# First MLP's up projection by one level of a Strassen scheme, with the activations at another 64-byte offset in SBUF

## The chip, the cores and the metric

The kernel runs on one core of a Trainium2 chip. The metric is device time in microseconds (us) of one execution. The kernel before was timed in three runs: 1188.42 to 1190.4 us, median 1188.81 us. Every time below comes from these runs or from the profile of one execution of the kernel before.

## What is computed

The program is a trunk of two layers over 512 positions of width 1024, in float32. Cut to what matters here:

```python
def sq_relu_mlp(h, w1, w2):
    return jnp.square(jax.nn.relu(h @ w1)) @ w2      # w1: 1024 x 4096, w2: 4096 x 1024

for i in range(2):
    hn = rmsnorm(h, norm_mix_g[i])
    h = h + (dsa_mixer(hn, ...) if i == 0 else conv_mixer(hn, ...))
    h = h + sq_relu_mlp(rmsnorm(h, norm_mlp_g[i]), mlp_w1[i], mlp_w2[i])
return rmsnorm(h, final_g)
```

Layer 0 is attention and an MLP ("the first MLP"), layer 1 a convolution mixer and an MLP ("the second MLP"). The change rewrites the first half of the first MLP, `h @ w1`.

## The kernel before

**Layout.** The residual `hT` lies transposed: 8 tiles of 128 features by 512 positions. A product of fp32 matrices is made of three TensorE matmuls on split operands (`mm3`, L90 to L93): each operand is a high part and a low part, hi·hi, hi·lo and lo·hi are summed in PSUM. The activations' parts are the tiles `ghi` and `glo`, written by `scaled` (ACT L174, DVE L175); the weights' parts are `whi` (ACT L86) and `wlo` (DVE L87), made by `split` for 512 columns of a weight tile at a time. `load` (L76) brings 1 MB of weights by SP's queue into `wraw`, a pool of two buffers.

**The first MLP.** It goes in four groups of 1024 hidden features. In a group `up_proj` makes 8 blocks of 128 features, each 8 k-steps of three matmuls of 512 columns into one PSUM bank; `hidden` turns a block into its square with relu and the rms factor (DVE L636, ACT L638 and L641, DVE L642) and leaves it as a pair `hh`, `hl`. Then `proj` makes the group's part of the down projection in 8 blocks, and DVE adds each to `hT` (L709). The factor `rr` of the rms norm is worked out after the first block or two (`rms_cols`, `broadcast`: DVE L181, POOL, DVE L190, four small matmuls, ACT L193), because it is applied to the result. Splits go to the pool `wsplit_mid`, 12 buffers for each of the two parts.

**What sets the order.** TensorE runs the blocks as the code writes them. A scheduler puts ACT's and DVE's work in order, by its own simulated times; each engine then takes its instructions strictly in that order, and a later one can't pass an earlier one that waits. SP's queue issues the loads in order; a load waits until the buffer that it fills has been read for the last time.

**Around it.** Before the first MLP stands the end of the attention layer: `wo_end` adds the last output blocks to `hT` (L617) and calls `scaled` for each feature tile. Behind group 0 stands `stacked_taps`, which builds the convolution's diagonal weights on POOL (L700). The pools `att` (attention) and `mlp` (first MLP) lie over the same memory. In SBUF all activations and weights start at a multiple of 512 bytes.

Of the kernel before, what the change touches and what calls it, by code (L numbers as in the profile page):

```python
# [42 lines left out]

ROW = 512
FILL = 64
# [3 lines left out]
def kernel(  # L49
# [29 lines left out]
    wsplit = []  # L79

# [19 lines left out]
    def bank(name="mm"):  # L100
        return acc.tile([P, S], F32, tag="mm", name=name)
# [36 lines left out]

    fill = small.tile([P, FILL // 4], F32, name="fill")
    nc.gpsimd.memset(fill, 0.0)  # L140
# [79 lines left out]
    with tc.tile_pool(name="wsplit_att", bufs=5) as ws, \  # L220
# [3 lines left out]
        wsplit.append(ws)  # L224
# [193 lines left out]
        with tc.tile_pool(name="heads", bufs=1) as heads:  # L418
# [86 lines left out]
            with tc.tile_pool(name="att_p", bufs=2) as att_p:  # L505
# [110 lines left out]
                def wo_end(c, ps):  # L616
                    nc.vector.tensor_add(hT[c], ps, hT[c])  # L617
                    scaled(c, vec("mlp", c))
                    rms_add(st, c)
# [42 lines left out]
    def pw1_first(k):  # L662

        for i, p in enumerate((aproj, gproj)):
# [9 lines left out]
    diags = [late.tile([P, max(TAPS0[c][0], TAPS1.get(c, (0, 0))[0]), 4, 32], F32, name=f"diag{c}")  # L674
             for c in range(KC)]

    def stacked_taps(pool):
# [3 lines left out]
        cw4 = pool.tile([P, 2 * P], F32, name="cw4")  # L681
        sel = pool.tile([P, 32], F32, name="sel")
# [4 lines left out]
        for i in range(2):  # L687
            r = pool.tile([P, 4, 32], F32, name=f"cwr{i}")
# [14 lines left out]
    with tc.tile_pool(name="mlp", bufs=1) as mlp:  # L703
        rr = []
        for g in range(NG - 1):
            hid = up_proj(mlp_w1[0][:, g * D:(g + 1) * D], rr, mlp, st if g == 0 else None)
            down = proj(mlp_w2[0][g * D:(g + 1) * D, :], hid)
            for c in range(KC):
                nc.vector.tensor_add(hT[c], down([c])[0], hT[c])  # L709
            if g == 0:  # L710
                stacked_taps(mlp)
        hid = up_proj(mlp_w1[0][:, DFF - D:], rr, mlp)
        down = proj(mlp_w2[0][DFF - D:, :], hid)
# [17 lines left out]
    HS = S // 2  # L731
    halves = [slice(0, HS), slice(HS, S)]
    with tc.tile_pool(name="cv", bufs=1) as cv, \
# [7 lines left out]
        with tc.tile_pool(name="cv_t", bufs=2) as cv_t:  # L741
# [14 lines left out]
            def taps(c, cs, npe, npool):  # L756
# [16 lines left out]
                sh4 = cv_t.tile([P, 4, S + 4 * (TAPS // 4 - 1)], F32, tag="sh4", name="sh4")  # L773
# [265 lines left out]
```

## Time and profile before

| | |
|---|---|
| runs | 1188.42 to 1190.4 us, median 1188.81 us |
| profiled execution, own time | 1186.75 us |
| its span, first to last instruction | 1185.0 us |
| busy: TensorE (PE), DVE, ACT, POOL | 97%, 56%, 42%, 21% of the span |
| the first MLP | 274 us to about 636 us |

PE is matmuls, DVE the vector engine, ACT the scalar engine, POOL GpSimd, SP the engine that issues most DMAs. A row of the timeline is start, duration, engine, line, operation, output<-inputs; a number at the end (x8) is a run of the same instruction, and square brackets give the idle time ahead of it and what ended it. The profiled execution's own time is 1.75 us above its span, and 2.06 us below the median of the runs.

### The profile page before, as it was taken

The page shows a single profiled execution, that of the slowest core. Times are in us where ns is not written, and L with a number is a line of the kernel's source. Part 1 is how long each engine was busy: PE and PEld are TensorE (multiplying, and loading weights), DVE is VectorE, ACT ScalarE, POOL GpSimd, SP SyncE. Part 2 cuts the span into 40 slices and gives each one's busy share as a digit, 9 for nine tenths or more (in the row PEclk, how much of TensorE's full clock was granted, in tenths as well). Part 3 has the DMA queues.
Part 4 walks back from the last instruction along what each step waited for, and adds up shares of the span by engine and source line. Part 5 has one row for each costly group of instructions (what it writes and reads, how often), then busy time and mean ns, then how long its engine had stood idle before and what let it go on. Part 6 is the DMA issues. An engine that isn't in the chain of part 4 may idle for free.

```text
span 1185.0 us, 15284 instructions
## 1 busy us (share of the span) xinstructions
PE 1150.8 (97%) x5828; PEld 948.5 (80%) x5828; DVE 663.3 (56%) x1195; ACT 498.2 (42%) x936; POOL 247.5 (21%) x248
## 2 busy tenths in 40 slices
PE   7999999999999999999999988899999999999997
PEld 6778888877888888888888666689888888888886
DVE  4589854476434434434444998878544434434434
ACT  5353454545423423423435544466632432432422
POOL 2436643322005000000012667632100000000000
PEclk8999999999999999999999998999999999999999
DMA  6122222215233323322323563533322332332211
GB/s 229 36 71 72 89 84 77 71 36 182 78 100 107 98 80 107 107 83 78 125 71 116 151 172 91 161 108 115 117 86 92 107 107 72 106 107 92 86 36 71
DMA packets 104353, 117.84 MB, mean 99 GB/s; under 512 B 3817, under 2 KB 87609, under 8 KB 104280
## 3 DMA queue, kind: packets, MB, share of 16 engines
q1 hardware_dynamic: 102440, 112.89, 30.6%
q10 hardware_dynamic: 1840, 3.97, 0.9%
q8 instruction: 46, 0.75, 0.3%
q14 instruction: 27, 0.22, 0.1%
HBM read 112.56 MB, written 4.29 MB: 99 GB/s over the span
## 4 chain that ended last, share of the span: by engine, by line
PE 81%; DVE 12%; DMA 2%; issue 2%; ACT 1%; POOL 1%; SPq 0%; POOLq 0%; DVEq 0%; ACTq 0%
PE mm L91 19%; PE mm L93 19%; PE mm L92 19%; PE dps L93 5%; PE dps L92 5%; PE dps L91 5%; DVE score L482 2%; DVE m L480 2%; DVE conv L802 2%; DVE wlo L87 2%; DVE pa L798 1%; PE vps L91 1%; PE vps L92 1%; PE vps L93 1%; DMA xs<-in_x_dram 1%
## 5 line engine op out<-in xcount | busy, mean ns | idle before, releaser
L86 ACT ACTIVATE whi<-wraw 128x512 fp32r<-128x512 f32 x378 | 234.6, 631 | 469.9 <-PE mm L92 317.1
L92 PE MATMUL mm<-glo,whi 128*128 128x512 f32 (+1 forms) x928 | 337.0, 365 | 1.2 <-DVE glo L175 1.2
L93 PE MATMUL mm<-ghi,wlo 128*128 128x512 f32 (+1 forms) x928 | 337.1, 365 | 0.0
L91 PE MATMUL mm<-ghi,whi 128*128 128x512 f32 (+1 forms) x928 | 334.6, 366 | 1.9 <-ACT whi L86 0.8
L87 DVE TENSOR_TENSOR wlo<-wraw,whi 128x512 fp32r<-128x512 f32 x325 | 233.5, 726 | 177.7 <-ACT whi L86 174.1
L92 PEld LDWEIGHTS mm<-glo,whi 128*128 128x128 f32 x928 | 175.0, 189 | 31.0 <-issue 2.4
L91 PEld LDWEIGHTS mm<-ghi,whi 128*128 128x128 f32 x928 | 173.1, 189 | 32.6 <-issue 2.8
L93 PEld LDWEIGHTS mm<-ghi,wlo 128*128 128x128 f32 x928 | 175.0, 189 | 28.7 <-issue 1.1
L93 PE MATMUL mm<-hh,wlo 128*128 128x512 f32 x256 | 99.6, 389 | 0.0
L92 PE MATMUL mm<-hl,whi 128*128 128x512 f32 x256 | 99.6, 389 | 0.0
L92 PE MATMUL dps<-wlo,hh 128*128 128x512 f32 x256 | 99.6, 389 | 0.0
L91 PE MATMUL mm<-hh,whi 128*128 128x512 f32 x256 | 99.1, 389 | 0.0
L91 PE MATMUL dps<-whi,hh 128*128 128x512 f32 x256 | 99.1, 389 | 0.0
L93 PE MATMUL dps<-whi,hl 128*128 128x512 f32 x256 | 98.6, 389 | 0.0
L636 DVE SCALAR_TENSOR_TENSOR hr<-mm,rmsb 128x512 f32<-128x512 f32 x64 | 44.1, 691 | 91.9 <-PE mm L93 90.2
L87 POOL TENSOR_TENSOR wlo<-wraw,whi 128x512 fp32r<-128x512 f32 x53 | 70.9, 1342 | 89.6 <-ACT whi L86 89.5
L183 POOL TENSOR_TENSOR fr<-v,mhalf 128x1 f32<-128x1 f32 x4 | 2.2, 548 | 340.2 <-DVE v L181 340.2
L642 DVE TENSOR_TENSOR hl<-hf,hh 128x512 fp32r<-128x512 f32 x64 | 44.6, 697 | 41.9 <-ACT hh L641 41.9
L206 POOL TENSOR_TENSOR ss<-sq 128x512 f32<-128x512 f32 (+1 forms) x4 | 5.7, 1434 | 270.3 <-ACT sq L201 270.3
L790 POOL TENSOR_TENSOR pa<-pa,pt 128x512 f32<-128x512 f32 (+1 forms) x43 | 53.6, 1249 | 32.6 <-ACT pt L788 30.5
L92 PEld LDWEIGHTS mm<-hl,whi 128*128 128x128 f32 x256 | 48.0, 188 | 10.1
L92 PEld LDWEIGHTS dps<-wlo,hh 128*128 128x128 f32 x256 | 48.0, 188 | 10.0
(257 smaller groups left out, 1588.2 us busy)
## 6 DMA issues: line engine op xcount, KB each, us to landing
wraw<-in_mlp_w_dram SPq DMA_DIRECT2D x64, 1024.0 KB, 5.2
wraw<-in_conv_w_pw_dram SPq DMA_DIRECT2D x12, 1024.0 KB
wraw<-in_dsa_w_in_dram SPq DMA_DIRECT2D x10, 1024.0 KB, 9.1
wraw<-in_dsa_w_out_dram SPq DMA_DIRECT2D x4, 1024.0 KB, 4.9
sh<-flat SPq DMA_DIRECT2D x12, 260.0 KB, 3.6
sh<-flat SPq DMA_DIRECT2D x20, 138.0 KB, 2.8
xw<-in_dsa_w_in_dram ACTq DMA_DIRECT2D x4, 584.0 KB, 7.4
xs<-in_x_dram SPq DMA_DIRECT2D x4, 512.0 KB, 12.1
```

The lines of the kernel that those rows point to most:

```text
L86: nc.scalar.activation(hi, src, AF.Copy)
L87: (eng or nc.vector).tensor_sub(lo, src, hi.bitcast(F32))
L91: nc.tensor.matmul(ps, wh, xh, start=start, stop=False)
L92: nc.tensor.matmul(ps, wh, xl, start=False, stop=False)
L93: nc.tensor.matmul(ps, wl, xh, start=False, stop=stop)
L480: nc.vector.max(m8s[-1], score[i])
L482: nc.vector.match_replace(score[i], m8s[i - 1], score[i], TAKEN)
L636: nc.vector.scalar_tensor_tensor(r, ps, 0.0, rr[0], op0=OP.max, op1=OP.mult)
L642: nc.vector.tensor_sub(tl, f, th.bitcast(F32))
L790: nc.gpsimd.tensor_add(pa, pa, pt)
L798: nc.vector.scalar_tensor_tensor(pa, sh(t), wt(t), pa, op0=OP.mult, op1=OP.add)
L802: nc.vector.scalar_tensor_tensor(cps, sh(t), wt(t), cps, op0=OP.mult, op1=OP.add)
```

## The change

A Strassen scheme multiplies two matrices of 2 by 2 blocks with 7 block products in place of 8. Here the blocks are: two of the hidden features (128 each), two halves of the 1024 inputs (4 tiles of 128 each), and two halves of the 512 positions. `pair` handles two feature blocks: 7 products of 4 k-steps by three matmuls of 256 columns (84 matmuls of 256 columns, where two blocks had 48 of 512). `two_pairs` interleaves two pairs, in TensorE's order p1, q5 (pair a), p1, q5 (pair b), then p2, p2, q6, q6, p7, p7, p3, p4, p3, p4. Its operands are sums: on the weights' side four (s1 to s4, DVE, `plain`, 512 columns), of which each is split like a weight; on the activations' side d1, e2, e3 and e4, worked out once before group 0 by `first_half` and `second_half`, which take over the work of `scaled`. The products of a pair are put together again through copies out of PSUM on ACT and sums on DVE.

```diff
-FILL = 64
+SHIFT = 64
+HS = S // 2
...
+    def wsplit_pool(stack, name, bufs, fill):
+        pool = stack.enter_context(tc.tile_pool(name=name, bufs=bufs, side="right"))
...
+        nc.gpsimd.memset(pool.tile([P, fill // 4], F32, tag="fill", name="fill", bufs=1), 0.0)
...
-    fill = small.tile([P, FILL // 4], F32, name="fill")
-    nc.gpsimd.memset(fill, 0.0)
...
                 def wo_end(c, ps):
                     nc.vector.tensor_add(hT[c], ps, hT[c])
-                    scaled(c, vec("mlp", c))
                     rms_add(st, c)
...
-    wsplit.append(ctx.enter_context(tc.tile_pool(name="wsplit_mid", bufs=12)))
+    wsplit_pool(ctx, "wsplit_mid", 12, 32 + ROW - SHIFT)
...
-            if g == 0:
-                stacked_taps(mlp)
...
+        def first_half(i):
+            w = mlp.tile([P, S], F32, tag="hh", name="xa", bufs=8)
+            x12 = mlp.tile([P, S], F32, tag="hl", name="x12", bufs=8)[:, t1]
+            nc.scalar.activation(w[:, t1], hT[i][:, t1], AF.Copy, scale=vec("mlp", i))
+            nc.scalar.activation(x12, hT[i][:, t2], AF.Copy, scale=vec("mlp", i))
+            nc.vector.tensor_sub(w[:, t2], w[:, t1], x12)
+            nc.scalar.activation(ghi[i], w, AF.Copy)
+            nc.vector.tensor_sub(glo[i], w, ghi[i].bitcast(F32))
...
+        def second_half(i, d1, x12):
+            c = i + 4
+            x = mlp.tile([P, S], F32, tag="hr", name="xb", bufs=2)
+            nc.scalar.activation(x, hT[c], AF.Copy, scale=vec("mlp", c))
+            nc.scalar.activation(ghi[c], x, AF.Copy)
+            nc.vector.tensor_sub(glo[c], x, ghi[c].bitcast(F32))
...
+            nc.vector.tensor_add(v[:, 0], d1, x[:, t2])
+            nc.vector.tensor_sub(v[:, 1], x12, x[:, t2])
+            nc.vector.tensor_sub(v4, x[:, t1], v[:, 0])
+            hi, lo = triple(2 * i), triple(2 * i + 1)
+            for src, at in ((v, slice(0, 2)), (v4.unsqueeze(1), slice(2, 3))):
+                nc.scalar.activation(hi[:, at], src, AF.Copy, scale=-1.0)
+                nc.vector.scalar_tensor_tensor(lo[:, at], src, -1.0, hi[:, at].bitcast(F32),
+                                               op0=OP.mult, op1=OP.subtract)
...
+        PRODUCTS = {"p1": ("a11", "b11"), "p2": ("a12", "b21"), "q5": ("s1", "d1"), "q6": ("s2", "e2"),
+                    "p7": ("s3", "e3"), "p3": ("s4", "b22"), "p4": ("a22", "e4")}
+        def pair(w, p):
+            raw = load(w, 0, KC, 2 * p * P, 2 * P)
...
+            def plain(name):
+                of = {"s1": ("a21", "a22"), "s2": ("s1", "a11"), "s3": ("a21", "a11"), "s4": ("s2", "a12")}
+                if name not in a:
+                    x, y = (plain(n) for n in of[name])
+                    a[name] = mlp.tile([P, 4, P], F32, tag="cs", name="cs", bufs=5)
+                    nc.vector.tensor_add(a[name], x, y)
+                return a[name]
...
+        def two_pairs(w, p, hid, between=lambda: None):
+            prods = [pair(w, p + z) for z in range(2)]
...
+            for z in range(2):
+                al[z] = half(bank("al"))
+                prods[z](al[z], "p1", True)
+                ga[z] = half(up_ps.tile([P, S], F32, tag="ga", name="ga"))
+                prods[z](ga[z], "q5", True)
+            between()
+            for z in range(2):
+                be[z] = half(bank("be"))
+                prods[z](be[z], "p2", True)
+                ua[z] = mlp.tile([P, S], F32, tag="ua", name="ua", bufs=2)
+                s = tmp.tile([P, S], F32, tag="sq", name="p1")[:, t1]
+                nc.scalar.activation(s, al[z], AF.Copy)
+                nc.vector.tensor_add(ua[z][:, t1], be[z], s)
+            for z in range(2):
+                prods[z](al[z], "q6", False)
+                s2[z] = tmp.tile([P, S], F32, tag="sq", name="s2")[:, t1]
+                nc.scalar.activation(s2[z], al[z], AF.Copy)
+            for z in range(2):
+                prods[z](al[z], "p7", False)
+                ub[z] = ut()
+                s = tmp.tile([P, S], F32, tag="sq", name="s3")[:, t1]
+                nc.scalar.activation(s, al[z], AF.Copy)
+                nc.vector.tensor_add(ub[z][:, t2], ga[z], s)
+            for z in range(2):
+                prods[z](ga[z], "p3", False)
...
+                prods[z](al[z], "p4", False)
...
+                for p in (0, 2):
+                    two_pairs(w1, p, hid, norm_rows if g == p == 0 else lambda: None)
...
+        stacked_taps()
```

`norm_rows` is `rms_cols` and `broadcast`. `xa`, `x12` and the sums lie in the pool `mlp`, so over the attention's memory; the last matmuls of the attention's output projection must be over before they are written. `hh` and `hl` have 8 buffers where they had 10. With `SHIFT` and the fills, `ghi`, `glo`, the e-operands, `hT` and `wraw` start at 448 modulo 512 bytes; the weights of `wsplit_mid` and `hh`, `hl` stay at 0. So the relative offset of the two operands is another for all products of the first MLP's up projection and for the other matmuls on `ghi` and `glo` with weights of `wsplit_mid`: 960 of 512 columns and 768 of 256.

The order on DVE at the start of the first MLP, before. The first row is the last addition of the attention layer, the last row the diagonals for `rr`.

```order
L617 TENSOR_TENSOR hT_103<-mm,hT_103 128x512
L87 TENSOR_TENSOR wlo<-wraw,whi 128x512 x8
L175 SCALAR_TENSOR_TENSOR glo_119<-hT_103,pv,ghi_111 128x512
L181 TENSOR_SCALAR v<-rms_ps 128x4
L87 TENSOR_TENSOR wlo<-wraw,whi 128x512 x2
L190 TENSOR_SCALAR diag<-ident,rms 128x128 x4
```

The same place in the change, the first rows behind the last addition and the last rows ahead of the diagonals. L737, L761 to L763 and L767 make the activations' sums and their low parts (`e_2844` is e2 and e3 side by side), L739 and L755 `glo`, L787 the weights' sums (`cs`), L99 is the low part of a weight.

```order
L627 TENSOR_TENSOR hT_101<-mm,hT_101 128x512
L737 TENSOR_TENSOR xa<-xa,x_2813 128x256
L737 TENSOR_TENSOR xa<-xa,x_2820 128x256
L737 TENSOR_TENSOR xa<-xa,x_2827 128x256
L737 TENSOR_TENSOR xa<-xa,x_2834 128x256
L761 TENSOR_TENSOR e_2844<-xa,xb 128x256
L762 TENSOR_TENSOR e_2844<-x_2813,xb 128x256
L763 TENSOR_TENSOR e_2845<-xb,e_2844 128x256
```

```order
L787 TENSOR_TENSOR cs<-cs,wraw 128x512
L99 TENSOR_TENSOR wlo<-cs,whi 128x512
L99 TENSOR_TENSOR wlo<-wraw,whi 128x512
L191 TENSOR_SCALAR v<-rms_ps 128x4
L99 TENSOR_TENSOR wlo<-cs,whi 128x512
L99 TENSOR_TENSOR wlo<-wraw,whi 128x512
L200 TENSOR_SCALAR diag<-ident,rms 128x128 x4
```

Between the last addition and the diagonals stand 11 rows before (10 low parts of weights and one `glo`) besides `v`; in the change 34 rows of 512 columns (8 `glo`, 4 low parts of e2 and e3, 8 weight sums, 14 low parts of weights) and 20 of 256 columns, besides `v`.

The order on DVE in a later group of the change, between the two halves of a group: `ua` and `hr` put the first two pairs together, `cs` and `wlo` from the row that waits for a DMA on belong to the next two pairs.

```order
L833 TENSOR_TENSOR ua<-be,p_3896 128x256 [waits PE_49]
L99 TENSOR_TENSOR wlo<-cs,whi 128x512 [waits Activation_49]
L833 TENSOR_TENSOR ua<-be,p_3917 128x256 [waits PE_49]
L787 TENSOR_TENSOR cs<-wraw 128x512 [waits DMAHW1_49]
L787 TENSOR_TENSOR cs<-cs,wraw 128x512
L99 TENSOR_TENSOR wlo<-wraw,whi 128x512 [waits Activation_49]
L787 TENSOR_TENSOR cs<-cs,wraw 128x512 [waits DVE_49]
L787 TENSOR_TENSOR cs<-wraw 128x512
L787 TENSOR_TENSOR cs<-wraw 128x512 [waits DVE_49]
L99 TENSOR_TENSOR wlo<-cs,whi 128x512 [waits Activation_49]
L99 TENSOR_TENSOR wlo<-wraw,whi 128x512 [waits PE_49,Activation_49] x2
L787 TENSOR_TENSOR cs<-cs,wraw 128x512 [waits DVE_49]
L99 TENSOR_TENSOR wlo<-cs,whi 128x512 [waits PE_49,Activation_49]
L843 TENSOR_TENSOR hr<-ga,s_3979 128x256 [waits Activation_49]
```

Before, DVE's rows at such a place alternate between a block's own results and the next block's low parts, two low parts to a block:

```order
L636 SCALAR_TENSOR_TENSOR hr<-mm,rmsb 128x512 [waits DVE_49,PE_49]
L87 TENSOR_TENSOR wlo<-wraw,whi 128x512 [waits Activation_49]
L642 TENSOR_TENSOR hl<-hf,hh 128x512 [waits Activation_49]
L87 TENSOR_TENSOR wlo<-wraw,whi 128x512 [waits DMAHW2_49,PE_49,Activation_49]
L636 SCALAR_TENSOR_TENSOR hr<-mm,rmsb 128x512 [waits DVE_49,PE_49]
```

In the change `hr<-ga`, the row that TensorE's eleventh product (p3) waits for since it goes on in the same PSUM bank, stands behind 11 rows of 512 columns, the first of which waits for a load.

## Rows read from the trace of the kernel before

**Rows 1.** The page: head, busy time of the engines, chain that ended last by engine.

```profile
span 1185.0 us, 15284 instructions
PE 1150.8 (97%) x5828; PEld 948.5 (80%) x5828; DVE 663.3 (56%) x1195; ACT 498.2 (42%) x936; POOL 247.5 (21%) x248
PE 81%; DVE 12%; DMA 2%; issue 2%; ACT 1%; POOL 1%; SPq 0%; POOLq 0%; DVEq 0%; ACTq 0%
```

**Rows 2.** Windows: opening, group 0's down projection, all of the first MLP.

```profile
core 0: us, PE busy (x) PEld busy (x) DVE busy (x) ACT busy (x) POOL busy (x), PEclk, DMA share, GB/s
274.00:290.70 16.70, 14.78 (x71) 11.84 (x71) 13.41 (x24) 10.53 (x19) 4.17 (x6) 1.00 0.59 182
...
330.00:373.60 43.60, 43.60 (x195) 36.04 (x194) 17.86 (x28) 11.58 (x19) 6.63 (x16) 1.00 0.30 97
...
274.00:636.00 362.00, 360.08 (x1595) 297.69 (x1595) 167.50 (x253) 135.45 (x223) 27.86 (x53) 1.00 0.32 102
```

**Rows 3.** Timeline of PE, 512-column matmuls; between the two rows stand 11 more.

```profile
399.64 0.39 PE L93 MATMUL mm<-ghi,wlo 128*128 128x512 f32 x1
...
402.36 0.39 PE L93 MATMUL mm<-ghi,wlo 128*128 128x512 f32 x1
```

**Rows 4.** Timeline of PE, 256-column matmuls (second layer); 32 stand between.

```profile
818.02 0.28 PE L93 MATMUL mm<-ghi,wlo 128*128 128x256 f32 x1
...
821.98 0.28 PE L92 MATMUL mm<-glo,whi 128*128 128x256 f32 x1
```

**Rows 5.** Timeline of DVE at the start of the first MLP.

```profile
274.12 0.69 DVE L617 TENSOR_TENSOR hT<-mm,hT 128x512 f32<-128x512 f32 x1 [3.21 <-PE mm L93]
274.83 4.96 DVE L87 TENSOR_TENSOR wlo<-wraw,whi 128x512 fp32r<-128x512 f32 x8
...
283.10 0.16 DVE L181 TENSOR_SCALAR v<-rms_ps 128x4 f32<-128x4 f32 x1 [1.61 <-PE rms_ps L215]
...
284.87 0.88 DVE L190 TENSOR_SCALAR diag<-ident,rms 128x128 f32<-128x128 f32 x4 [0.31 <-POOL rms L183]
285.66 3.10 DVE L87 TENSOR_TENSOR wlo<-wraw,whi 128x512 fp32r<-128x512 f32 x5
```

**Rows 6.** Timeline of DVE, 256-column operations (second layer); three stand between.

```profile
808.24 0.42 DVE L860 TENSOR_TENSOR u<-u,dr 128x256 f32<-128x256 f32 x1
...
809.58 0.42 DVE L862 TENSOR_TENSOR glo<-u,ghi 128x256 fp32r<-128x256 f32 x1
```

**Rows 7.** Timeline of PE in the opening.

```profile
281.54 0.50 PE L92 MATMUL mm<-glo,whi 128*128 128x512 f32 x1 [1.15 <-DVE glo L175]
...
282.11 0.95 PE L215 MATMUL rms_ps<-ones,ss 128*128 128x1 f32 x8
```

**Rows 8.** Groups by line and shape: busy us, mean ns of one, idle before.

```profile
L86 ACT ACTIVATE whi<-wraw 128x512 fp32r<-128x512 f32 x378 | 234.6, 631 | 469.9 <-PE mm L92 317.1 <-PE dps L93 103.1 <-PE vps L93 11.8
L87 DVE TENSOR_TENSOR wlo<-wraw,whi 128x512 fp32r<-128x512 f32 x325 | 233.5, 726 | 177.7 <-ACT whi L86 174.1 <-PE mm L92 2.3 <-PE rms_ps L191 0.9
L858 ACT ACTIVATE ghi<-u 128x256 fp32r<-128x256 f32 x16 | 6.7, 416 | 0.4
L700 POOL TENSOR_TENSOR diag<-sel,cw 128x128 f32<-128x128 f32 x33 | 15.3, 502 | 82.1 <-DVE cw L696 82.1
```

**Rows 9.** Loads: the page's DMA part (1 MB each, us to landing), then waits of SP's queue.

```profile
wraw<-in_mlp_w_dram SPq DMA_DIRECT2D x64, 1024.0 KB, 5.2
```

```profile
SPq L76 <- DVE wlo L87: 704.4, 75, 27.8
SPq L76 <- DMA wraw<-in_mlp_w_dram: 9.8, 3, 5.0
```

**Rows 10.** Windows in the second layer: TensorE starved, then the stretch behind.

```profile
676.00:684.00 8.00, 5.47 (x23) 3.71 (x21) 7.96 (x13) 5.84 (x11) 7.41 (x5) 1.00 0.75 178
684.00:687.40 3.40, 3.08 (x16) 0.92 (x20) 3.40 (x4) 0.63 (x1) 3.32 (x4) 0.50 0.31 92
```

More of the change, by code (lines that the diff above doesn't have):

```diff
@@ L44 @@
 ROW = 512
-FILL = 64
+SHIFT = 64
+HS = S // 2
+LATE = ((5,), (6,), (7,), (0, 2), (1, 4), (3,))
 @with_exitstack
@@ L79 @@
     wsplit = []
+    def wsplit_pool(stack, name, bufs, fill):
+        pool = stack.enter_context(tc.tile_pool(name=name, bufs=bufs, side="right"))
+        for part in ("whi", "wlo"):
+            nc.gpsimd.memset(pool.tile([P, S], F32R, tag=part, name=part).bitcast(F32), 0.0)
+        nc.gpsimd.memset(pool.tile([P, fill // 4], F32, tag="fill", name="fill", bufs=1), 0.0)
+        wsplit.append(pool)
     def split(src, eng=None, pool=None, tag="w", bufs=None):
@@ L219 @@
     w_in = dsa_w_in[0]
-    with tc.tile_pool(name="wsplit_att", bufs=5) as ws, \
+    with ExitStack() as ws, \
             tc.tile_pool(name="att", bufs=1) as att, \
             tc.tile_pool(name="att_ps", bufs=2, space=PSUM) as att_ps:
-        wsplit.append(ws)
+        wsplit_pool(ws, "wsplit_att", 5, 32)
         def lg():
@@ L669, in pw1_first, with stacked_taps @@
                 pw1.extend(ps)
-    wsplit.append(ctx.enter_context(tc.tile_pool(name="wsplit_mid", bufs=12)))
+    wsplit_pool(ctx, "wsplit_mid", 12, 32 + ROW - SHIFT)
     conv_ctx = ExitStack()
     late = conv_ctx.enter_context(tc.tile_pool(name="late", bufs=1))
[L674 to L682, printed above, removed]
+    diags = {}
+    def stacked_taps():
+        for i, cc in enumerate(LATE):
+            ns = [max(TAPS0[c][0], TAPS1.get(c, (0, 0))[0]) for c in cc]
+            t = late.tile([P, sum(ns), 4, 32], F32, tag=f"late{i}", name=f"diag{i}")
+            for c, n in zip(cc, ns):
+                diags[c] = t[:, :n]
+                t = t[:, n:]
+        t = tmp.tile([P, S], F32, tag="sq", name="cw4")
+        cw4, sel = t[:, :2 * P], t[:, 2 * P:2 * P + 32]
         nc.gpsimd.tensor_add(sel, ident[:, 0:32], ident[:, 32:64])
@@ L687, in stacked_taps @@
         for i in range(2):
-            r = pool.tile([P, 4, 32], F32, name=f"cwr{i}")
+            r = tmp.tile([P, S], F32, tag="sq", name="cwr")[:, :P].rearrange("p (s i) -> p s i", s=4)
             if i:
@@ L728 @@
             table(AF.Sigmoid, ghi[KC - 1].bitcast(F32))
-    HS = S // 2
     halves = [slice(0, HS), slice(HS, S)]
@@ L772, in taps @@
                 nc.sync.dma_start(flat, sh(0, w + 3 - n))
-                sh4 = cv_t.tile([P, 4, S + 4 * (TAPS // 4 - 1)], F32, tag="sh4", name="sh4")
+                sh4 = cv_t.tile([P, 4, S + 12], F32, tag="sh4", name="sh4")
                 for z in range(4):
@@ L944 @@
             tc.tile_pool(name="m2_ps", bufs=2, space=PSUM) as m2_ps:
+        m2_fill = m2.tile([P, SHIFT // 4], F32, name="m2_fill")
+        nc.gpsimd.memset(m2_fill, 0.0)
         fg = m2.tile([P, D], F32, name="fg")
```

71 lines of the change are left out of this document (63 added, 8 removed).

## The prediction

> **What bounds the kernel now.** I read the page's head first: TensorE is busy for 97% of the span, and the chain that ended last runs through it for 81% [rows 1]. The windows then show the first MLP by itself: 362.00 us, of which TensorE is idle 1.92, all of it in the opening (16.70 long, 14.78 busy), while DVE works 167.50 and ACT 135.45 [rows 2]. So here fewer columns on TensorE save time one to one, as long as the other engines keep ahead of it; and a wait that is added to TensorE costs its full length.
>
> **TensorE's own work.** Two blocks of features take 48 matmuls of 512 columns now, and 84 of 256 in the change. From start to start a 512-column matmul takes (402.36 − 399.64)/12 = 0.2267 us [rows 3], a 256-column one (821.98 − 818.02)/33 = 0.120 us [rows 4]; the halves are not half as long, since at 2.4 GHz the columns alone are 0.2133 and 0.1067, and 13.3 ns are left over in both. A pair goes from 48 × 0.2267 = 10.88 to 84 × 0.120 = 10.08, so it saves 0.80 us, and the 16 pairs save **12.8 us**. The Trainium skill, "TensorE: Matmul & The Clock Gate", section "Back-to-back issue gap", gives N/2.4 + 2.5 ns as the gap of one isolated matmul, so 109 and 216 ns, by which the saving would be about 19 us. The trace disagrees with it (120 and 227), and the sum goes by the trace.
>
> **The opening.** The activations' sums lie in memory that the attention holds until its last output matmul, so they all start where the last addition to hT stands. From there to the diagonals for the rms factor DVE's queue has 34 operations of 512 columns and 20 of 256 (11 of 512 before). Back to back, one of 512 takes (3.10 − 0.69)/4 = 0.602 us (five in a row; eight in a row give 0.61) [rows 5], one of 256 (809.58 − 808.24)/4 = 0.335 [rows 6]. So 34 × 0.602 + 20 × 0.335 + 0.16 + 0.88 for `v` and the diagonals = 28.2 us. In this time TensorE has only the four products p1, q5, p1, q5, 48 × 0.12 = 5.8 us, and the rms sums, 0.95 [rows 7]; p2 stands behind the diagonals in its order. Its idle time is 28.2 − 6.7 = 21.5, less the 1.9 of today 19.6. If no operation overlaps the one behind it, 0.69 and 0.42 each make 32.9 us, and 24.3 for the idle time. I take **+21**: near the lower end, as eight in a row do keep the spacing, with two copies on ACT of 0.63 [rows 8] that DVE must wait for in the chain hT, scaled copy, sum, high part, low part.
>
> **The first group's second load.** The loads of the next two pairs can start only when DVE has read the raw weights for the last time, about 0.9 us ahead of the diagonals' end. The median landing is 5.2 us behind the issue [rows 9]; DVE's queue waits for it there, then has 11 operations of 512 columns and one of 256 ahead of the row that releases TensorE's product p3: 11 × 0.602 + 0.42 = 7.0, and 0.4 for the row itself. That is 5.2 − 0.9 + 7.4 = 11.7 us behind the diagonals. TensorE's six products from p2 to p7 take 6 × 1.44 = 8.6. The wait is 3 us; with 0.726 for each operation [rows 8] 4.4. I take **+4**, nearer the upper end, as both loads are under way at once.
>
> **Later groups, between their halves.** The same row order returns in groups 1 to 3. The last split of the first two pairs (the 14th) needs a buffer, and with 12 it is that of the second product, done 2.9 us into the group; with ACT's 0.63 and DVE's 0.69 behind it the next load starts at 4.2, lands at 9.4, and DVE's rows up to the release take 7.0: 16.4. TensorE has ten products ahead of p3, 14.4 us. It waits 2.0; with 0.726 an operation 3.4. I take 2.7 for each of three groups, **+8.1**. What is queued behind the waiting row on DVE are the group's own results, so none of it can be moved forward; SP's queue has nothing else to do.
>
> **The halves that follow.** There the next loads are those of the down projection, which need no sums on DVE. But ACT has four high parts (4 × 0.63) ahead of the copy of q6, which p7 waits for; the copy itself is 0.42 [rows 8], and TensorE has one product, 1.44, in hand: 2.5 + 0.4 − 1.4 = 1.5 at worst, nothing if the load is early. I take 1.0 for each of four, **+4** (0 to 6).
>
> **The clock.** Behind a stretch with 2.5 us of idle time in 8 the granted clock was 0.50 for 3.4 us, that is 1.2 for 2.4 GHz [rows 10]. Behind an opening in which TensorE idles for most of 28 us I expect such a stretch once: half of 3.4, **+1.7** (0 to 3.4).
>
> **Costed at nothing.** The move of `stacked_taps` behind the last group: its 15.3 us on POOL [rows 8] run beside the last down projection, which like group 0's gives TensorE 43.60 us without a gap [rows 2]; without that cover it would add up to 15. The scaled parts that leave the end of the attention were off TensorE's path; ACT's copies for the sums have DVE's queue as the longer one beside them; eight buffers for `hh` in place of ten just hold a group.
>
> **Sum.** −12.8 + 21 + 4 + 8.1 + 4 + 1.7 = +26.0. The profiled execution took 1186.75, its span 1185.0 and 1.75 around it; the change gives 1212.8 by it. The median of the runs is 2.06 above that execution, so the forecast is **1215** as a median, 26 above 1188.81. With all lower ends (−12.8 + 19.6 + 3 + 6.0 = +15.8) it is 1205, with all upper ones (−12.8 + 24.3 + 4.4 + 10.2 + 6 + 3.4 = +35.5) 1224.
>
> **The rivals.**
> *The offset takes the 13.3 ns away* (ends on the other side). In before all operands start at the same offset modulo 512 bytes, and every form that I read has this leftover [rows 3, 4]; in the change the activations are shifted against the weights. If the leftover comes from that, it goes for 1728 matmuls outside the new products, 23 us, all on TensorE's path, and for the 1344 new ones, 17.9 us, of which I count half, since where TensorE waits for DVE a faster matmul only waits longer. 26 − 23 − 9 = −6: **1183**, faster. It decides from about four fifths of the leftover on (26 of 32). For it: the columns alone don't explain the spacing. Against: no row of before has two operands at different offsets, so nothing shows that the offset matters. The Trainium skill, "SBUF — State Buffer", section "Who interferes with whom", says that TensorE's two read ports, for the moving operand and for the weights, are independent; by that rule the offset changes nothing, and no row here shows it. Chance 0.17.
> *Only the opening costs.* If loads land sooner than 5.2, or DVE's rows behind them overlap ACT better than I count, the waits between halves vanish: −12.8 + 21 + 1.7 = +9.9, **1199**. For it: TensorE is never short in the groups of today [rows 2]. Against: DVE has 19 rows for a pair of blocks (7 low parts, 4 sums, 8 for the results) where it has 8. Chance 0.13.
> *More waits, or a larger leftover.* If the shift doubles the leftover, 32 us come on top: 1247. If the loads land late in half of the seven places behind the opening, by the 5.0 that a load waited for another [rows 9], 17 come on top: 1232. Together **1224 to 1247**, chance 0.12.
> *The opening is covered after all*, because the sums start during the attention's last blocks: −12.8 alone, **1176**. Against: the memory and DVE's order both forbid it. Chance 0.03.
>
> **How the numbers follow.** My forecast has 0.55 (1205 to 1224). A measurement of this kernel can tell 0.2%, about 2.4 us, from no change. Faster: most of the first rival and the last, 0.18; within 0.2%: the rest of the first rival, 0.04; slower: 0.78. The range 1184 to 1240 leaves out the last rival, about half of the first and the upper part of the third, some 0.17. As both signs are in it, the forecast's own range stands above.
>
> **What would show it.** In the changed kernel's profile: start to start of 256-column matmuls in the up projection (0.120 if the offset is neutral, 0.107 to 0.109 for the first rival), and of 512-column ones in the second MLP and the convolution's projection; TensorE idle for some 20 us in the opening with DVE named as its releaser; idle time ahead of p3 in each group, ended by `hr<-ga`; a window with clock 0.50 behind the opening. The prediction is wrong if DVE gets through the opening in much less than 28 us, if p2 doesn't stand behind the diagonals, or if the matmuls' spacing is another.

## The result and the profile after

The changed kernel took 1221.41 us (median of 4 runs, 1219.48 to 1223.21) where the kernel before took 1188.62 in the same comparison: a ratio of 1.0274, with an interval of [1.0251, 1.0297], so 32.8 us slower. The forecast was 1215. The profiled execution of the change took 1219.48 us for a span of 1217.7.

The page of the changed kernel, its head, busy times and chain, against [rows 1]:

```profile
span 1217.7 us, 16772 instructions
PE 1146.9 (94%) x6404; PEld 962.9 (79%) x6404; DVE 755.3 (62%) x1395; ACT 542.5 (45%) x1052; POOL 249.9 (21%) x255
PE 70%; DVE 15%; DMA 9%; issue 3%; ACT 3%; SPq 1%; POOL 0%; POOLq 0%; ACTq 0%; DVEq 0%
```

TensorE's busy time fell by only 3.9 us, and the chain that ended last, which ran through TensorE for 81%, does so for 70%: most of the difference went to DMA (9% for 2%) and DVE (15% for 12%). The windows say where, against [rows 2] (the opening; the rest of group 0's up projection; group 1's up projection; the first MLP):

```profile
core 0: us, PE busy (x) PEld busy (x) DVE busy (x) ACT busy (x) POOL busy (x), PEclk, DMA share, GB/s
275.30:309.00 33.70, 12.29 (x63) 11.26 (x63) 30.33 (x60) 22.77 (x45) 4.91 (x6) 0.67 0.08 24
309.00:347.60 38.60, 36.53 (x293) 35.91 (x293) 29.98 (x56) 21.96 (x44) 0.00 (x0) 0.94 0.45 144
391.90:436.30 44.40, 40.96 (x338) 39.98 (x337) 33.14 (x61) 24.14 (x49) 0.00 (x0) 1.00 0.44 142
275.30:666.00 390.70, 355.83 (x2172) 316.45 (x2172) 263.78 (x460) 184.47 (x347) 30.20 (x57) 0.97 0.30 95
```

The opening is the picture that was forecast: DVE is busy for 30.3 of 33.7 us while TensorE idles for 21.4. The granted clock of 0.67 there says that part of TensorE's work ran slowly; the section on the prediction comes back to it. In group 1, 44.4 us hold 41.0 of TensorE, and the idle 3.4 us eat what the scheme takes off. The waits of TensorE, largest first (in total, times, longest; those of the second layer left out), name the same places:

```profile
PE ga L796 <- ACT whi L98: 7.3, 1, 7.3
PE ga L796 <- DVE hr L843: 7.0, 4, 2.1
PE al L796 <- ACT ghi L738: 6.2, 1, 6.2
PE bc L201 <- DVE diag L200: 4.7, 1, 4.7
PE al L796 <- ACT s L837: 3.5, 6, 1.5
```

The third, the first and the fourth are the opening, in this order of time: ahead of p1 for the first operand, ahead of q5 for the high part of the first weight sum, ahead of the broadcast for the diagonals. The second is p3 behind `hr<-ga`, once in each group; the fifth is p7 behind the copy of q6.

The next table divides both spans into places. They are bounded by the start of the attention's last addition to `hT` and the starts of the first and last matmul of each down projection (us):

| | before | change | difference |
|---|---|---|---|
| start to last addition of the attention | 274.1 | 275.4 | +1.3 |
| group 0, up | 48.0 | 72.2 | +24.2 |
| groups 1 to 3, up (three together) | 131.5 | 130.8 | -0.7 |
| the four down projections | 181.3 | 186.2 | +4.9 |
| behind the first MLP | 550.1 | 553.1 | +3.0 |
| span | 1185.0 | 1217.7 | +32.7 |

Three quarters are group 0's up projection, with the opening in it. But 9 us are in places in which the prediction had nothing: ahead of the first MLP, in the down projections and behind the first MLP.

The other view to look at is the spacing of matmuls. The timeline of PE in the changed kernel, two 256-column stretches of the up projection (18 and 17 matmuls stand between) and a 512-column stretch of the second MLP (12 between), against [rows 3, 4]:

```profile
327.73 0.28 PE L796 MATMUL al<-ghi,whi 128*128 128x256 f32 x1
...
329.89 0.28 PE L796 MATMUL ga<-glo,whi 128*128 128x256 f32 x1
...
421.06 0.28 PE L796 MATMUL be<-ghi,whi 128*128 128x256 f32 x1
...
423.18 0.28 PE L796 MATMUL be<-ghi,whi 128*128 128x256 f32 x1
...
879.75 0.39 PE L103 MATMUL mm<-ghi,whi 128*128 128x512 f32 x1
...
882.78 0.39 PE L104 MATMUL mm<-glo,whi 128*128 128x512 f32 x1
```

The first is (329.89 - 327.73)/19 = 0.1137 us, the second (423.18 - 421.06)/18 = 0.1178, where 256 columns took 0.120; the third is (882.78 - 879.75)/13 = 0.2331 where 512 columns took 0.2267. Both widths have changed, and with opposite signs. That it is the offset, and the one between the two operands, two things show: the first experiment, and the attention of the same kernel, where activations and weights both start at 448 modulo 512 bytes. There 512 columns still take (152.97 - 150.25)/12 = 0.2267 (11 rows between):

```profile
150.25 0.39 PE L103 MATMUL mm<-ghi,whi 128*128 128x512 f32 x1
...
152.97 0.39 PE L103 MATMUL mm<-ghi,whi 128*128 128x512 f32 x1
```

### The profile page after: what moved, and what is told of

Read it like the earlier page. It is cut to its first block, busy times and chain, and to the rows that moved or that the text cites. A ratio compares the mean times of both kernels' runs of the same rounds, so it can differ in the third digit from the quotient of the medians.

```text
span 1217.7 us, 16772 instructions
## 1 busy us (share of the span) xinstructions
PE 1146.9 (94%) x6404; PEld 962.9 (79%) x6404; DVE 755.3 (62%) x1395; ACT 542.5 (45%) x1052; POOL 249.9 (21%) x255
## 4 chain that ended last, share of the span: by engine, by line
PE 70%; DVE 15%; DMA 9%; issue 3%; ACT 3%; SPq 1%; POOL 0%; POOLq 0%; ACTq 0%; DVEq 0%
PE mm L104 14%; PE mm L103 14%; PE mm L105 14%; PE dps L105 5%; PE dps L104 5%; PE dps L103 5%; DMA wraw<-in_mlp_w_dram 5%; DVE wlo L99 4%; PE al L796 2%; DVE pa L956 1%; PE vps L103 1%; PE vps L105 1%; PE vps L104 1%; DMA sh<-flat 1%; PE conv L938 1%
## 5 line engine op out<-in xcount | busy, mean ns | idle before, releaser
L98 ACT ACTIVATE whi<-wraw 128x512 fp32r<-128x512 f32 x362 | 222.0, 627 | 375.2 <-PE mm L104 190.1
L99 DVE TENSOR_TENSOR wlo<-wraw,whi 128x512 fp32r<-128x512 f32 x309 | 224.0, 735 | 150.6 <-ACT whi L98 146.7
L104 PE MATMUL mm<-glo,whi 128*128 128x512 f32 (+1 forms) x672 | 237.8, 356 | 0.2 <-DVE glo L185 0.2
L105 PE MATMUL mm<-ghi,wlo 128*128 128x512 f32 (+1 forms) x672 | 237.8, 356 | 0.0
L103 PE MATMUL mm<-ghi,whi 128*128 128x512 f32 (+1 forms) x672 | 235.1, 357 | 0.7 <-ACT rmsb L203 0.7
L104 PEld LDWEIGHTS mm<-glo,whi 128*128 128x128 f32 x672 | 126.1, 188 | 21.6 <-issue 2.1
L103 PEld LDWEIGHTS mm<-ghi,whi 128*128 128x128 f32 x672 | 124.1, 188 | 23.5 <-issue 2.8
L105 PEld LDWEIGHTS mm<-ghi,wlo 128*128 128x128 f32 x672 | 126.0, 188 | 20.5 <-issue 1.1
L99 POOL TENSOR_TENSOR wlo<-wraw,whi 128x512 fp32r<-128x512 f32 x53 | 70.1, 1327 | 90.6 <-ACT whi L98 90.6
L796 PE MATMUL al<-e,whi 128*128 128x256 f32 x384 | 69.2, 281 | 3.6 <-ACT s L837 3.5
L98 ACT ACTIVATE whi<-cs 128x512 fp32r<-128x512 f32 x64 | 40.3, 630 | 64.6 <-PE mm L104 43.9
L796 PEld LDWEIGHTS al<-e,whi 128*128 128x128 f32 x384 | 58.3, 188 | 5.2 <-ACT s L837 5.2
L948 POOL TENSOR_TENSOR pa<-pa,pt 128x512 f32<-128x512 f32 (+1 forms) x43 | 53.9, 1257 | 32.8 <-ACT pt L946 30.8
## 6 DMA issues: line engine op xcount, KB each, us to landing
xs<-in_x_dram SPq DMA_DIRECT2D x4, 512.0 KB, 12.8
```

The source lines that it names most:

```text
L98: nc.scalar.activation(hi, src, AF.Copy)
L99: (eng or nc.vector).tensor_sub(lo, src, hi.bitcast(F32))
L103: nc.tensor.matmul(ps, wh, xh, start=start, stop=False)
L104: nc.tensor.matmul(ps, wh, xl, start=False, stop=False)
L105: nc.tensor.matmul(ps, wl, xh, start=False, stop=stop)
L796: nc.tensor.matmul(ps, l[:, k, :], r, start=start and k == n == 0, stop=k == 3 and n == 2, skip_group_check=not start)
```

## The experiments

All times are medians; each ratio is against the kernel before, run on the same chip.

### 1. The offset back, and the offset alone

The changed kernel with every operand at a multiple of 512 bytes again:

```diff
+    fill = small.tile([P, SHIFT // 4], F32, name="fill0")
+    nc.gpsimd.memset(fill, 0.0)
...
-        wsplit_pool(ws, "wsplit_att", 5, 32)
+        wsplit_pool(ws, "wsplit_att", 5, 32 + ROW - SHIFT)
...
-        mlp_fill = mlp.tile([P, SHIFT // 4], F32, name="mlp_fill")
...
-        m2_fill = m2.tile([P, SHIFT // 4], F32, name="m2_fill")
```

> The changed kernel with all activations and weights back at a multiple of 512 bytes; nothing else moves. Of the two widths: the trace of the change shows 256-column matmuls at 0.113 to 0.118 us start to start (0.120 before) and the 512-column ones whose relative offset is new at 0.231 to 0.234 (0.2267 before). Theory 1 (the spacing belongs to the relative offset, with opposite sign for the two widths): 256 columns return to 0.120 and 512 to 0.2267. That is 2112 x 0.0045 = +9.5 us, of which the 1344 new ones (6.0) partly vanish in waits, and 960 x 0.006 = -5.8: +1 to +4, so about 1223 to 1225. Rival (the new spacings come from other work beside them, more DVE and ACT traffic): the spacings stay and the time stays at 1221. Rival (the offset is what made the change slow): the time falls by over 5.

1215.15 us (1210.59 to 1218.55), ratio 1.0225 [1.0203, 1.0248]: 6 us faster than the change, not 1 to 4 slower, so in the time the last of the three readings came true. The spacings went back as Theory 1 said. This kernel's timeline of PE has (330.95 - 327.83)/26 = 0.120 in the up projection (25 rows between), and (882.85 - 879.68)/14 = 0.2264 in the same place of the second MLP (13 rows between):

```profile
327.83 0.28 PE L796 MATMUL ga<-glo,whi 128*128 128x256 f32 x1
...
330.95 0.28 PE L796 MATMUL ga<-ghi,whi 128*128 128x256 f32 x1
...
879.68 0.39 PE L103 MATMUL mm<-ghi,whi 128*128 128x512 f32 x1
...
882.85 0.39 PE L105 MATMUL mm<-ghi,wlo 128*128 128x512 f32 x1
```

What was wrong is the account of what they are worth. In the first MLP the 1344 new matmuls lost their gain, yet the four up projections together took 203.2 us against 203.0 in the change: TensorE had only been waiting longer. Meanwhile the 512-column matmuls' loss counts in full: the last three up projections of the second MLP took 45.03 us each in the change and take 43.75 here. By the places of the table the 6.0 us between the two profiled executions are 1.3 ahead of the first MLP (the last addition is back at 274.1), 2.1 in the down projections (184.2 here) and 2.9 behind the first MLP (550.2). The 2.1 aren't the spacing, as both operands of a down projection start at a multiple of 512 bytes in both kernels; their cause is open.

The kernel before with the same offset and nothing else:

```diff
-    fill = small.tile([P, FILL // 4], F32, name="fill")
-    nc.gpsimd.memset(fill, 0.0)
...
     wsplit.append(ctx.enter_context(tc.tile_pool(name="wsplit_mid", bufs=12)))
+    fill = wsplit[-1].tile([P, FILL // 4], F32, name="fill", bufs=1)
+    nc.gpsimd.memset(fill, 0.0)
```

> The kernel before with the offset alone: ghi, glo, hT, wraw at 448 modulo 512 bytes, the weights behind the attention, hh and hl at 0; no Strassen scheme. 1728 matmuls of 512 columns and 768 of 256 get the new relative offset. Theory 1: 1728 x 0.006 = +10.4, 768 x 0.0045 = -3.5, so +7: about 1195.5, slower than before. Rival of the prediction (the new offset takes the 13.3 ns left over away): 2496 x 13.3 ns = -33, about 1155. Rival (no part of it): 1188.6.

1198.96 us, ratio 1.0091 [1.0077, 1.0105]: slower by 10.8 us, so Theory 1's sign holds and the prediction's rival, in which the offset takes the leftover away, is dead; the size is 4 us more than the expectation's 7. Part of that is ahead of the first MLP: the last addition of the attention came at 274.9 (274.1 before). The page's DMA part of this kernel shows loads that land later into the shifted tiles, 12.9 for `xs` where before has 12.1, 7.9 for `xw` where it has 7.4, 5.4 for `wraw` where it has 5.2 [rows 9]:

```profile
wraw<-in_mlp_w_dram SPq DMA_DIRECT2D x64, 1024.0 KB, 5.4
xw<-in_dsa_w_in_dram ACTq DMA_DIRECT2D x4, 584.0 KB, 7.9
xs<-in_x_dram SPq DMA_DIRECT2D x4, 512.0 KB, 12.9
```

The pages of the other kernels agree. In the five with the offset, the changed one among them, `xs` has 12.8 to 13.0, `xw` 7.9 to 8.4 and `wraw` 5.3 to 5.4, and the last addition stands at 274.9 to 275.4; in the seven without it they are 12.1 to 12.3, 7.3 to 7.6, 5.0 to 5.2, and 273.9 to 274.5. That the later landings make the early part longer is read from these numbers side by side; no run separates it.

### 2. Less work for DVE in the opening

The changed kernel without the operands e2 to e4:

```diff
-            nc.vector.tensor_add(v[:, 0], d1, x[:, t2])
-            nc.vector.tensor_sub(v[:, 1], x12, x[:, t2])
-            nc.vector.tensor_sub(v4, x[:, t1], v[:, 0])
...
-            for z, name in enumerate(("e2", "e3", "e4")):
-                xop[name, i] = hi[:, z], lo[:, z]
+            for name in ("e2", "e3", "e4"):
+                xop[name, i] = xop["b21", i]
```

> The changed kernel without the work for e2, e3 and e4: their sums and parts aren't made, and the products that would read them read the parts of the block b21 in their place (a part of the computation is left out). TensorE has the same matmuls. In the opening DVE loses 12 sums and 4 low parts of 256 columns and 4 low parts of 512: 16 x 0.335 + 4 x 0.602 = 7.8 us. Theory 2 (the opening lasts as long as DVE's queue): the idle time of TensorE there falls by 7 to 8, the time to about 1213.5. Rival (the opening is set by memory that comes free late, by ACT or by the loads): under 3 of it comes back, 1218 or more.

1214.73 us, ratio 1.0236 [1.0209, 1.0263]: 6.7 us less for 7.8 us of DVE's work. From the last addition to the first down matmul group 0 took 62.1 us for 72.2, more than was taken from DVE, and groups 1 to 3 up took 136.7 for 130.8; the longer part there wasn't traced. So that DVE's queue sets the opening is borne out, while the agreement of 6.7 with 7.8 is partly chance.

### 3. The weight sums on POOL

```diff
-                    nc.vector.tensor_add(a[name], x, y)
+                    nc.gpsimd.tensor_add(a[name], x, y)
```

> The changed kernel with the 64 weight sums (plain) on POOL in place of DVE, in all groups. Theory 2: the opening falls by 8 x 0.6 = 4.8, since POOL makes the sums at once beside DVE's other work; between the halves of a group DVE's rows behind the load fall by 6 x 0.6 = 3.6, so the waits ahead of p3 (2 in each group) and most of those ahead of p7 go: about -4.8 - 4 x 2 - 3 = -16, 1205 to 1209. Rival (the waits between halves come from the loads or from ACT, not from DVE's queue): only the opening's 4.8, 1216 to 1217. Rival (POOL slows DVE's operations or its longer sums, some 1.3 us each in a chain s1, s2, s4, come too late): 1221 or slower.

1241.89 us, ratio 1.045 [1.0436, 1.0464]: 20 us slower than the change, the last of the expectation's rivals. The groups by line show why. The sums take 1.55 to 1.64 us on POOL (0.68 on DVE in the change), and the low parts that DVE makes beside them 0.935 for 0.682. In the change the groups are these:

```profile
L787 DVE TENSOR_TENSOR cs<-wraw 128x512 f32<-128x512 f32 x32 | 21.5, 686 | 22.0 <-DMA wraw<-in_mlp_w_dram 22.0
L99 DVE TENSOR_TENSOR wlo<-cs,whi 128x512 fp32r<-128x512 f32 x64 | 43.5, 682 | 19.4 <-ACT whi L98 19.4
```

With the sums on POOL they are the first two lines below, and TensorE's wait for `hr<-ga`, the third, grew from 7.0 to 17.8 us:

```profile
L787 POOL TENSOR_TENSOR cs<-wraw 128x512 f32<-128x512 f32 x32 | 52.0, 1637 | 196.6 <-DMA wraw<-in_mlp_w_dram 178.6 <-DVE wlo L99 12.1 <-DVE e L767 5.9
L99 DVE TENSOR_TENSOR wlo<-cs,whi 128x512 fp32r<-128x512 f32 x64 | 59.5, 935 | 22.1 <-ACT whi L98 21.4
```

```profile
PE ga L796 <- DVE hr L843: 17.8, 5, 4.3
```

The Trainium skill, "SBUF — State Buffer", section "Who interferes with whom", says that a DVE instruction with two inputs in SBUF contends with a GpSimd instruction that reads SBUF. DVE's row agrees, 0.935 us beside POOL's sums for 0.682 without them; no run shows POOL's sums with DVE idle.

### 4. Group 0 without the scheme

This experiment starts from the first experiment's kernel (offset back). Group 0's up projection goes as in the kernel before, without the Strassen scheme, and the operands of the scheme are made behind it, from `ghi` and `glo`:

```diff
 def wo_end(c, ps):
     nc.vector.tensor_add(hT[c], ps, hT[c])
+    scaled(c, vec("mlp", c))
...
-            parts = [first_half(i) for i in range(4)]
-            for i in range(4):
-                second_half(i, *parts[i])
...
+                if g == 0:
+                    hid = up_proj(w1, rr, mlp, st, bufs=8)
+                    for i in range(4):
+                        operands(i)
```

> Start is the changed kernel with the offset back (e1_offset_back, 1215.2). Group 0's up projection goes as in the kernel before (48 matmuls of 512 columns a pair, the scaled parts made at the end of the attention), and the activations' sums are made from ghi and glo under group 0's down projection; groups 1 to 3 keep the Strassen scheme. Theory 2 (nearly all of the loss is the opening, where DVE's queue stood in front of TensorE): group 0 from the last addition to its first down matmul goes from 72.8 back to about 48.0, the sums hide under a down projection in which DVE is idle for over half the time, and the rest stays: 1215.2 - 24.8 = 1190.4, between 1189 and 1193. Rival (the sums are a cost wherever they are, since DVE and ACT are the bound in the first MLP): the down projection of group 0 or the start of group 1 grows by 5 or more, 1196 or slower. Rival (the groups 1 to 3 gain what TensorE saves, 3.2 each): 1180.

1189.95 us, ratio 1.0019 [1.001, 1.0028]: 25.2 us less than the kernel that it starts from, as expected (1190.4). The sums do hide. In the windows of this kernel group 0's down projection is full of TensorE while DVE has nearly twice the work of [rows 2]; and group 1's up projection still has its 3 us of idle time:

```profile
324.60:368.00 43.40, 43.40 (x193) 35.93 (x193) 34.55 (x67) 16.36 (x30) 0.00 (x0) 1.00 0.15 49
368.00:412.40 44.40, 41.32 (x339) 40.68 (x338) 33.49 (x62) 24.78 (x50) 0.00 (x0) 1.00 0.43 142
```

### 5. The load between the halves

This kernel is that of experiment 4, but the second half of each group of the scheme reads the first half's raw weights again, so the loads in the middle of a group are left out:

```diff
+            if p < 2:
+                raws[p] = load(w, 0, KC, 2 * p * P, 2 * P)
-            raw = load(w, 0, KC, 2 * p * P, 2 * P)
+            raw = raws[p % 2]
```

> As e5_group0_plain, but the second half of each Strassen group reads the raw weights of the first half again: the two loads between the halves are left out (so the second half multiplies by other weights than the reference's), all else stays, the same splits and sums on the same engines. Theory 4 (the waits ahead of p7 and p3 in the middle of a group, 2.3 to 3.3 us each time, come from the load that DVE and ACT wait for, with the current results queued behind): they fall under 0.5, the time by 6 to 9 against e5_group0_plain. Rival (they come from the number of DVE's rows alone): they stay within 1 us, the time within 2 of e5_group0_plain.

1182.14 us, ratio 0.9955 [0.9943, 0.9968]: 7.8 us less than the kernel of experiment 4. TensorE's waits for `hr<-ga`, in the kernel of experiment 4 and in this one:

```profile
PE ga L790 <- DVE hr L837: 5.5, 5, 1.7
```

```profile
PE ga L794 <- DVE hr L841: 1.1, 5, 0.2
```

They fell from 5.5 us in all to 1.1, with the same operations on DVE. So it is the load on which DVE's queue stands, not the number of rows behind it alone. In the changed kernel this is seen row by row. The next three fences are the timelines of SP's queue, DVE and PE in group 1 (TensorE began the group at 392.2):

```profile
393.68 0.37 SPq L80 DMA_DIRECT2D wraw<-in_mlp_w_dram  x1
396.51 0.37 SPq L80 DMA_DIRECT2D wraw<-in_mlp_w_dram  x1
```

```profile
399.70 0.69 DVE L787 TENSOR_TENSOR cs<-wraw 128x512 f32<-128x512 f32 x1 [3.21 <-DMA wraw<-in_mlp_w_dram]
...
402.55 0.69 DVE L787 TENSOR_TENSOR cs<-wraw 128x512 f32<-128x512 f32 x1 [0.24 <-DMA wraw<-in_mlp_w_dram]
...
409.18 0.41 DVE L843 TENSOR_TENSOR hr<-ga,s 128x256 f32<-128x256 f32 x1
```

```profile
405.11 0.51 PE L796 MATMUL al<-e,whi 128*128 128x256 f32 x2 [1.48 <-ACT s L837]
409.65 0.38 PE L796 MATMUL ga<-ghi,whi 128*128 128x256 f32 x1 [1.54 <-DVE hr L843]
```

The loads are issued 1.5 and 4.3 us into the group, when the raw buffers come free, and land 6.0 us later; DVE idles 3.21 us for the first of them with TensorE's results waiting behind it in its queue, then needs 6.6 us from the second one's landing to `hr<-ga`; 0.5 behind that starts p3.

### 6. The last raw reader early

This is the kernel of experiment 4 again, with its loads, and the split of a22, the last row that reads a pair's raw weights, is issued ahead of p2's split instead of last (TensorE's order stays):

```diff
-                hi, lo = split(plain(wn))
+                hi, lo = early.pop(wn, None) or split(plain(wn))
...
             between()
+            for z in range(2):
+                prods[z].early("a22")
```

> As e5_group0_plain (1190.0), and the last split that reads a pair's raw weights, that of a22 for p4, is made early: it is issued ahead of p2's split for both pairs, TensorE's order stays. The two raw buffers then come free without waiting for a split buffer of the same group, and the loads of the next two pairs start before the group does. Theory 4 (those loads, 4 us into the group, are what makes TensorE wait at p7 and p3): nearly all that leaving the loads out gave (7.8 us) is there with the computation whole: 1182 to 1184, faster than the kernel before. Rival (the loads then collide with others or DVE's and ACT's other rows are late): 1187 or more.

1184.17 us, ratio 0.9956 [0.9943, 0.997]: faster than the kernel before by about 5 us, and than the change by 37, at the upper end of what was expected (1182 to 1184). In SP's queue a load of group 1's second half stands at 360.79, ahead of the group's start at 366.5, where the kernel of experiment 4 issued its two at 369.70 and 372.58 for a start at 368.0. The window of group 1 has 41.15 of 41.60 us on TensorE:

```profile
360.79 0.37 SPq L80 DMA_DIRECT2D wraw<-in_mlp_w_dram  x1
```

```profile
366.50:408.10 41.60, 41.15 (x339) 40.67 (x338) 34.77 (x63) 26.32 (x52) 0.00 (x0) 1.00 0.31 102
451.30:492.90 41.60, 41.15 (x339) 40.67 (x339) 34.90 (x63) 26.31 (x52) 0.00 (x0) 1.00 0.30 102
```

The next kernel has the change's offset on top:

```diff
-    fill = small.tile([P, SHIFT // 4], F32, name="fill0")
...
+        mlp_fill = mlp.tile([P, SHIFT // 4], F32, name="mlp_fill")
```

> As e10_early_a22 with the change's offset (activations at 448 modulo 512 bytes). Theory 1 by the measured spacings: 1008 matmuls of 256 columns in the first MLP and 768 behind it gain 4.5 ns each, 8.0 us; 1152 of 512 columns lose 6.3 ns each, 7.3 us; the start of the program and the loads lose 1 to 2 us as with the offset alone. With the waits gone the gain in the first MLP counts in full: 0 to +2 against e10_early_a22. Rival (the gain of 256-column matmuls never reaches the time, as in the change, where the group's ups were no shorter with it): +5 to +6.

1188.25 us, ratio 0.9999 [0.999, 1.0008]: 4 to 5 us more, between the two expectations. The gain of the 256-column matmuls is there now: groups 1 to 3 up took 124.4 us where they took 126.8. It is less than what the rest loses, 2.9 us behind the first MLP, 1.4 in group 0 with its 512 columns, and 1.0 ahead of it. So the rival's sum is nearer, for another reason than the rival's.

### 7. The taps

The first kernel here is the kernel before with `stacked_taps` behind the last up projection:

```diff
-            if g == 0:
-                stacked_taps(mlp)
...
         down = proj(mlp_w2[0][DFF - D:, :], hid)
+        stacked_taps(mlp)
```

> The kernel before with stacked_taps alone moved from behind group 0 to behind the last up projection. The prediction costed this at nothing. In the change the last down projection with what is in it took 53.2 to 53.6 us where it took 51.5. Theory 3 (the two transposes of the taps stand in TensorE's queue ahead of the first down matmul and wait for their DMAs and buffers): the last down projection grows by 1 to 2 us, 1190. Rival (the 1.7 us come from the last up projection's late results, not from the taps): within 0.5 us of before, 1188.

1187.84 us, ratio 1.0003 [0.9994, 1.0011]: the rival's number; the move alone costs nothing. The second is the kernel of experiment 4 with the taps behind one block of the last down projection:

```diff
-        stacked_taps()
...
                 if c:
                     pw1_first(c - 1)
+                else:
+                    stacked_taps()
```

> As e5_group0_plain, with stacked_taps behind the first block of the last down projection. Theory 3: the wait for the taps' DMAs vanishes under the block's 24 matmuls; 1 to 2 us less than e5_group0_plain, about 1188.5 to 1189.5. Rival (the cost is in the up projection's late results): no difference.

1201.88 us, ratio 1.0116 [1.01, 1.0132]: 12 us slower than the kernel of experiment 4, where 1 to 2 us less were expected. Windows and waits of this kernel show TensorE with 0.79 us of work in 7, waiting twice for the taps' DMAs, which stand in SP's queue only from 590.35 on, and behind that a granted clock of 0.73 (a mean of its two levels):

```profile
592.20:599.20 7.00, 0.79 (x4) 0.22 (x4) 2.04 (x3) 1.87 (x3) 0.20 (x1) 0.77 0.41 121
599.20:606.00 6.80, 6.80 (x23) 5.49 (x24) 1.14 (x2) 0.63 (x1) 5.77 (x15) 0.73 0.01 4
```

```profile
PE cw_ps L712 <- DMA cwr<-in_conv_w_dw_dram: 6.2, 2, 3.2
```

TensorE takes the transposes in their order, so they are no cheaper in the middle of the work if their data are issued later too. In the changed kernel the buffers are part of it: there the taps lie in the pool `tmp`, in the buffers of `sq`, and SP's queue held their load back for 4.1 us until DVE had read such a buffer. TensorE then waited 1.2 us for it, just ahead of the first down matmul, which stands at 611.05. The rows are from the waits of SP's queue and from PE's timeline:

```profile
SPq L707 <- DVE ua L846: 4.1, 1, 4.1
```

```profile
610.99 0.30 PE L709 MATMUL cw_ps<-ident,cwr 128*128 128x128 f32 x1 [1.22 <-DMA cwr<-in_conv_w_dw_dram]
```

In the places of the table this wait belongs to group 3's up projection. The wait isn't fixed: with the same buffers it is 0.23 us in the first experiment's kernel and under 0.1 in that of experiment 4. Whether other buffers would remove it was not tried. The kernel of experiment 6 has it, 1.13 us at the same place, and behind another of 1.16 for `hr<-ga` its group 3 up took 43.8 us where groups 1 and 2 took 41.5. The last down projection itself took 2.1 us more in the change than before; 0.7 of it are waits for `hl`, and the rest wasn't traced.

## Why the prediction was right, and where it was off

The main mechanism was the one forecast: DVE's queue stands in front of TensorE in the opening, and DVE's queue on a load in the later groups. The closeness of the sum is partly luck, as the terms show.

- **TensorE's own work** (-12.8): right at one offset. With the offset back 256 columns take 0.120 in the up projection too.
- **The opening** (+21), **the second load** (+4), the half behind it (+1) and **the clock** (+1.7), with group 0's share of the saving (-3.2), make +24.5 for group 0's up projection; it was +24.2. Here errors cancel. From the end of the last addition (276.1) to the end of the diagonals (308.2) DVE took 32.1 us, not 28.2; 2.5 of that were waits for copies on ACT and a row on POOL, for which +21 in place of 19.6 had left 1.4. TensorE's idle time of 21.4 matches the 21.5 of the working only because TensorE's own part was longer too: the first 32 of the 48 matmuls of its four products ran at a granted clock of 0.50 (1.2 of 2.4 GHz, behind 6.2 us in which TensorE stood idle), while DVE was the one to wait for. Behind the diagonals less was lost than the 6.7 forecast: p3 of the first half waited for 2.1, the longest of its kind, the half behind it didn't wait, and the clock was at 0.50 until 313.8, so that the first 20 of p2's matmuls took 4.4 us, about 2 more than at 0.117 each. The rows are DVE's timeline and two windows:

```profile
275.40 0.69 DVE L627 TENSOR_TENSOR hT<-mm,hT 128x512 f32<-128x512 f32 x1 [4.75 <-PE mm L105]
...
307.32 0.87 DVE L200 TENSOR_SCALAR diag<-ident,rms 128x128 f32<-128x128 f32 x4 [0.91 <-POOL rms L193]
```

```profile
281.54:300.17 18.63, 8.10 (x33) 7.21 (x34) 18.63 (x35) 13.15 (x25) 1.29 (x1) 0.50 0.00 0
307.66:313.80 6.14, 6.14 (x29) 6.14 (x29) 2.95 (x7) 1.86 (x3) 0.00 (x0) 0.50 0.90 298
```

- **Later groups**: forecast -3.2 + 2.7 + 1.0 for each, +0.5; with the offset back it was -0.4 (43.5 us for 43.8). The mechanism was the one named, shown by leaving the load out and by issuing it earlier: `hr<-ga` behind a load in DVE's queue. The copy of q6 on ACT that I put into the following half waited for in the same one (1.48 us in group 1), together with it; the following half waited 0.4.
- **The offset** is the step that failed. The prediction had it at nothing, with rivals in which it gave or took up to 32 us. It costs about 6 us of the change's 32.8. Of these 2.9 lie behind the first MLP, where 960 matmuls of 512 columns take 0.233 for 0.2267 us, on TensorE's path, and 768 of 256 gain 2 to 6 ns each; 1.3 lie ahead of it, beside the later landings, and 2.1 are in the down projections, whose cause is open. The gain of the 1344 matmuls in the first MLP went into the waits.
- **The sum.** With the offset back the change is at 1215.15, where the sum stood (1215). That this is so exact is luck: the down projections took 2.8 us more than before, for which the sum has no term, and groups 1 to 3 took 2.6 less than their terms.
- **Costed at nothing**: the taps' move costs nothing by itself; with the buffers that the change gives them TensorE waited 1.2 us for their load, and 0.2 with the offset back; the removed scaled parts cost nothing at the end of the attention (274.1 to the last addition before and with the offset back), and were part of the opening, as counted.
- **The rivals**: the offset's gain fell with experiment 1, the hidden opening with the profile. "Only the opening" was refuted by experiment 5, which got 7.8 us out of the groups. Late loads in half of the places, or a doubled leftover, didn't come: the longest wait for `hr<-ga` was 2.1 us, and the spacing of 512 columns grew by 6 ns.

## What to carry to other kernels

In this kernel a scheme that takes products from TensorE and gives sums to DVE paid only where DVE's sums had a stretch of TensorE's work to hide under: with the sums behind one group of the old form the kernel was 25 us faster than with the sums in front of the first product. In DVE's queue, which runs in order, a row that waits for a load holds back the results behind it. So look for the last reader of the load's buffer and issue it early: that gave 5.8 us here, while moving the sums to POOL lost 20. More buffers weren't tried. Price an alignment change for every width of matmul that it touches, and count the gain only where TensorE isn't waiting.

## What the runs showed of the hardware

The spacing of matmuls depends on the offset between the moving operand and the weights in SBUF. With the moving operand 64 bytes below a multiple of 512 and the weights at a multiple, 256 columns went from 0.120 to between 0.113 and 0.118 us and 512 columns from 0.2267 to 0.233. With both 64 bytes below, 512 columns stayed at 0.2267. Why is not shown. The Trainium skill, "SBUF — State Buffer", section "Who interferes with whom", has the two read ports of TensorE as independent; the measurement differs from what I took from it, that the offset can't matter. Loads into tiles at that offset landed 0.2 to 0.8 us later (pages of before and of experiment 1's second kernel). A float32 addition of 128x512 that takes 0.68 us on DVE took 1.6 on POOL and made DVE's own operations beside it a third slower.
